# Products of the v and output projections that hand over PSUM banks run two token tiles at a time

## The chip, the cores and the metric

The kernel runs on one core of one Trainium2 chip. The metric is the device time of one execution in microseconds (us). Inside a core, TensorE (PE) multiplies matrices into PSUM banks, VectorE (DVE), ScalarE (ACT) and GpSimd (POOL) work on tiles, and SyncE (SP) issues most of the DMAs. Each engine takes its instructions in one fixed order and stops at the first one whose inputs or buffers are not ready.

## The reference

One layer of a decoder over 1024 tokens of width 2048: a projection into head groups, sparse attention (group A), mLSTM (group B), the projection of both groups' outputs, and a normalisation. The two parts that the change touches are the columns `v_m` of the first projection and the product with `w_out`:

```python
proj = x @ w_in[l]
(q_a, c_kv, z_a, q_i, k_i, w_i, q_m, k_m, v_m,
 i_m, f_m, o_m, z_m) = jnp.split(proj, offs, axis=-1)
...
h_m = mlstm_chunkwise(q_m.reshape(B, T, H_M, DK_M), k_m.reshape(B, T, H_M, DK_M),
                      v_m.reshape(B, T, H_M, DV_M), i_m + b_igate[l], f_m + b_fgate[l])
...
y = jnp.concatenate([y_a, y_m], axis=-1) @ w_out[l]
x = layer_norm(ALPHA * x + y, ln_g[l], ln_b[l])
```

## The kernel before

Every float32 factor is split into a high part (`wh`, `xh`; a cast to fp32r on ScalarE) and a low part (`wl`, `xl`; a subtraction on VectorE), and three matmuls (high x high, low x high, high x low) stand for one product of 128 x 128 by 128 x 512.

**v.** `Values` computes the 1024 x 1024 block v = x times 2048 rows of weights. `run(False)` takes the first half of the 2048 rows and `run(True)` the second, each as a scheme with seven products instead of eight for 2 x 2 blocks of 512: `b11`, `b21`, `t1`, `t2`, `b22`, `t3`, `t4`, in that order. The factor is a block of weights or a sum of blocks: `t` is a buffer of four weight tiles to which a block is added on VectorE (L847) before `t2` and again before `t4`. Each product is 4 weight tiles (k) x 4 tiles of 128 tokens (t) x 3 matmuls = 48 matmuls at L861, into four PSUM banks, one per token tile. The banks are `pj` (for b11, t2, t3, t4), `pb` (b21) and `pc` (t1, b22); pb and pc are taken from the same four banks. After a product, `add` empties its banks into `v`, by ScalarE copies in the first pass where the block is new and by VectorE additions (L889) otherwise. So t1 can begin only when the additions of pb are done, and t4 when those of t3's pj are.

`product` has two orders. With `by_tile` it asks for all four weights and then runs tile after tile; without, it runs weight after weight, and for each weight all four tiles. b11 and t4 run by tile.

There are four buffers each for `wh` and `wl` (`WB`), and six for `wraw`, the weights as loaded (`WR`).

Beside this VectorE has a search for the attention's threshold and the mask built from it: an equality test `eq` (L653), a scan (L656) and three more passes (L659, L662, L666) for each block of 128 queries, whose length grows from 384 to 1024.

**Output projection.** `Product` does the same with `w_out` and the rows of y: three units of seven products (`unit_0`, `unit_1`, `unit_2`) at L1489, banks `lps`, `pb` and `pc`, additions into `z` at L1521 and L1523, ScalarE copies and scalings at L1525 and L1527. The y factors (`ya11`, `ys1`, `ys2` and others) are also split, by L108 on ScalarE and L109 on VectorE. Here b21 and t4 run by tile.

What each engine does first is settled by a scheduler that goes over the whole program with priorities (`urgent`, `out_prio`) and an estimate of each instruction's time, and writes out one order for each engine. A change of the order in which a product asks for its matmuls therefore moves instructions on the other engines too.

Of the kernel before, what the change touches and what calls it, by code (L numbers as in the profile page):

```python
# [102 lines left out]
def kernel(ctx, tc, a, out):  # L103
# [90 lines left out]
    def bank(name, shape=(P, 512)):  # L194
        return ss.tile(list(shape), F32, name=name, tag="b")
# [45 lines left out]
    for k in range(4):  # L241
        r, ws, xs = {}, [], []
# [154 lines left out]
    w, low = {}, {}  # L397
# [49 lines left out]
    with tc.high_priority(offset=I_PRIO), tc.issue_after(marks[n + 42].ins):  # L447
        for h in range(2):
            ps = bank("knt")
# [20 lines left out]
    with tc.high_priority(offset=I_PRIO), tc.issue_after(marks[n + 46].ins):  # L470
        for j in range(2):
            cn = s4("cn")
            for h in range(2):
                ps = bank("cnt")
# [6 lines left out]
        for h in range(2):  # L481
            ps = bank("gnt")
# [211 lines left out]
    class Unit:  # L694
# [53 lines left out]
        def product(self, ps, wname, xname, start):  # L748
            wh, wl = self.weights(wname)
            fh, fl = self.X[xname]  # L750
            for k in range(4):
                for n, (w, x) in enumerate(((wh, fh), (wh, fl), (wl, fh))):
                    last_mm[0] = pe.matmul(ps, w[:, k], x[:, k], start=start and k == 0 and n == 0,  # L753
                                           stop=k == 3 and n == 2, skip_group_check=True)
                if k % 2:
                    marks.append(last_mm[0])
# [57 lines left out]
    class Values:  # L814
# [11 lines left out]
        def run(self, second, X):  # L826
            k0 = 8 * second
            t_sum = x_tile("t", dt=F32)
            with urgent():
                for k in range(4):  # L830
                    self.load(t_sum[:, k], k0 + k, 1, (k0 + k, 0))

            def raw(k, n, more=None):
                return self.load(wp.tile([P, 512], F32, name="wraw", tag="wraw", bufs=WR), k, n, more)

            def weights(name, k):
                with urgent():
                    if name in ("b11", "b21"):
                        src = raw(k0 + 4 * (name == "b21") + k, 0)
                    elif name == "b22":  # L840
                        src = raw(k0 + 4 + k, 1)
                    elif name == "t3":
                        src = raw(k0 + 4 + k, 1, (k0 + k, 1))
                    else:
                        src = t_sum[:, k]
                        if name != "t1":
                            vec.tensor_tensor(src, src, raw(k0 + 4 + k, int(name == "t2")), op=OP.add)  # L847
                    wh = wp.tile([P, 512], F32R, name="wh", tag="wh", bufs=WB)
                    wl = wp.tile([P, 512], F32R, name="wl", tag="wl", bufs=WB)
                    last_cast[0] = act.copy(wh, src)  # L850
                    last_low[0] = vec.tensor_tensor(wl, src, wh.bitcast(F32), op=OP.subtract)
                search_on()
                return wh, wl

            def product(ps, wname, xname, start, by_tile=False):
                fh, fl = X[xname]

                def part(t, k, w):
                    ts = slice(t * P, (t + 1) * P)
                    for n, (x, y) in enumerate(((fh, w[0]), (fl, w[0]), (fh, w[1]))):  # L860
                        last_mm[0] = pe.matmul(ps[t], x[:, k, ts], y, start=start and k == 0 and n == 0,  # L861
                                               stop=k == 3 and n == 2, skip_group_check=True)
                    if t % 2:
                        marks.append(last_mm[0])

                if by_tile:
                    ws = [weights(wname, k) for k in range(4)]
                    for t in range(4):
                        for k in range(4):
                            part(t, k, ws[k])  # L870
                else:
                    for k in range(4):
                        w = weights(wname, k)
                        for t in range(4):
                            part(t, k, w)

            def block(i, n):
                self.c[i, n] = [s4("v", (P, 2, 512)) for _ in range(2)]
                if second:
                    with urgent():  # L880
                        for v in range(2):
                            sync.dma_start(self.c[i, n][v], v_d[n, i, :, 2 * v:2 * v + 2])

            def add(i, n, ps, first=False, minus=False, last=False):
                for t in range(4):
                    dst = self.c[i, n][t // 2][:, t % 2]
                    with urgent():
                        if not first or second:
                            vec.tensor_tensor(dst, dst, ps[t], op=OP.subtract if minus else OP.add)  # L889
                        elif minus:  # L890
                            act.mul(dst, ps[t], -1.0)
                        else:
                            act.copy(dst, ps[t])
                    if last and t % 2:
                        sync.dma_start(v_d[n, i, :, t - 1:t + 1], self.c[i, n][t // 2])

            pa = [pj() for _ in range(4)]
            block(0, 0)
            product(pa, "b11", "a11", True, True)
            add(0, 0, pa, True)  # L900
            pb = [bank("pb") for _ in range(4)]
            block(1, 1)
            product(pb, "b21", "a12", True)
            add(0, 0, pb, last=True)
            pc = [bank("pc") for _ in range(4)]
            product(pc, "t1", "s1", True)
            add(1, 1, pc, True)
            block(0, 1)
            product(pa, "t2", "s2", False)
            add(0, 1, pa, True, True)  # L910
            product(pc, "b22", "s4", False)
            add(0, 1, pc, last=True)
            block(1, 0)
            product(pa, "t3", "s3", False)
            add(1, 1, pa, minus=True, last=True)
            product(pa, "t4", "a22", False, True)
            add(1, 0, pa, True, last=True)


# [344 lines left out]
    with ExitStack() as ph:  # L1264
# [14 lines left out]
        for t in range(7, -1, -1):  # L1279
            w = max((t + 1) * P, 256)  # L1280
# [5 lines left out]
        for t in range(8):  # L1286
            m = mask[t]
            w = max((t + 1) * P, 256)
# [146 lines left out]
    class Product:  # L1435
# [44 lines left out]
                    pool.dma_start(src, a["wo"][c, :, k0 + 4], accum_op=OP.add)  # L1480
            return wh, wl

        def product(self, ps, wname, xname, start, by_tile=False):
            fh, fl = Y[xname]

            def part(t, k, w):
                ts = slice(t * P, (t + 1) * P)
                for n, (x, y) in enumerate(((fh, w[0]), (fl, w[0]), (fh, w[1]))):
                    pe.matmul(ps[t], x[k][:, ts], y, start=start and k == 0 and n == 0,  # L1489
                              stop=k == 3 and n == 2, skip_group_check=True)  # L1490

            with tc.issue_after(last_logit[0].ins):
                if by_tile:
                    ws = [self.weights(wname, k) for k in range(4)]
                    for t in range(4):
                        for k in range(4):
                            part(t, k, ws[k])
                else:
                    for k in range(4):
                        w = self.weights(wname, k)  # L1500
                        for t in range(4):
                            part(t, k, w)

        def block(self, i, n):
            if self.p:
# [29 lines left out]
        def run(self, then, following=None):  # L1535
            pa = [lps() for _ in range(4)]
            self.block(0, 0)
            self.product(pa, "b11", "a11", True)
            self.add(0, 0, pa, True, True)
            then("a11")  # L1540
            pb = [bank("pb") for _ in range(4)]
            self.product(pb, "b21", "a12", True, True)
            self.add(0, 0, pb, last=True)
            then("a12")
            self.block(1, 1)
            pc = [bank("pc") for _ in range(4)]
            self.product(pc, "t1", "s1", True)
            self.add(1, 1, pc, True)
            then("s1")
            self.block(0, 1)  # L1550
            self.product(pa, "t2", "s2", False)
            self.add(0, 1, pa, True)
            then("s2")
            self.product(pc, "b22", "s4", False)
            self.add(0, 1, pc, last=True)
            then("s4")
            nxt = following and Product(*following)
            self.block(1, 0)
            self.product(pa, "t3", "s3", False)
            self.add(1, 1, pa, last=True)  # L1560
            then("s3")
            self.product(pa, "t4", "a22", False, True)
            self.add(1, 0, pa, True, True, last=True)
            then("a22")
            return nxt
# [47 lines left out]
    for t in range(8):  # L1613
# [5 lines left out]
        for n in range(2):  # L1619
            ps = bank("zps") if t % 2 else lps()  # L1620
# [59 lines left out]
```

## Time and profile before

| | |
|---|---|
| median of 3 runs | 1834.79 us (1834.2 to 1838.15) |
| the profiled execution | 1842.1 us |
| its span (first to last instruction) | 1840.3 us |
| granted TensorE clock, mean | 0.99 |

The span is the time between the first and the last instruction of the profiled execution; 1.8 us of its time lie outside. Times in the rows further down count from the span's start. "Idle before" is the time that an engine did nothing ahead of an instruction, and behind the arrow stands what ended it.

### The profile page before, as it was taken

To read this page: it belongs to the slowest core of one execution; us is meant where nothing else is said; L and a number is where in the kernel's file an instruction comes from. 1 tells how busy PE (TensorE), PEld (TensorE's weight loads), DVE (VectorE), ACT (ScalarE), POOL (GpSimd) and SP (SyncE) were. 2 spreads that over 40 slices of the span, in tenths; PEclk is the share of its full clock that TensorE was granted. 3 is DMA by queue.
4 is the path that set the end of the run, shared out by engine and by line. 5 is a ranking of instruction groups with operands and counts; after the bars stand their busy time and mean duration, and the time that the engine had idled before them with its cause. 6 is when DMAs were issued, how large, how long until landed. Compare 5 with 4: busy or idle time off the path is not lost. (4 is left out here: it accounts for less than half of the span.)

```text
span 1840.3 us, 25485 instructions
## 1 busy us (share of the span) xinstructions
PE 1779.2 (97%) x8613; PEld 1497.0 (81%) x8613; DVE 1400.6 (76%) x2674; ACT 942.4 (51%) x1728; POOL 263.9 (14%) x316
## 2 busy tenths in 40 slices
PE   8899999999999999999999998999899999999997
PEld 8788888887888888777888887878788987888886
DVE  8766677767887768786878786877898976676777
ACT  6343266556666657321555564565665665333410
POOL 3101110000100010000101010010445531011000
PEclk9999999999999999999999999999999999999998
DMA  9886264445475667975666656466675448874764
GB/s 327 321 294 195 86 169 116 111 122 144 132 202 152 163 169 241 306 229 159 200 179 179 204 144 179 113 196 186 215 222 141 125 107 238 264 189 121 191 183 147
DMA packets 148732, 338.82 MB, mean 184 GB/s; under 512 B 16104, under 2 KB 25576, under 8 KB 142456
## 3 DMA queue, kind: packets, MB, share of 16 engines
q1 hardware_dynamic: 121880, 280.16, 46.1%
q0 software_dynamic: 26720, 57.03, 16.4%
q8 instruction: 68, 1.11, 0.2%
q14 instruction: 64, 0.52, 0.1%
HBM read 259.40 MB, written 91.35 MB: 191 GB/s over the span
## 5 line engine op out<-in xcount | busy, mean ns | idle before, releaser
L753 PE MATMUL pj<-xh,wh 128*128 128x512 f32 x960 | 376.3, 393 | 6.3 <-DVE res L762 4.5
L753 PE MATMUL pj<-xl,wh 128*128 128x512 f32 x960 | 375.2, 391 | 0.0
L753 PE MATMUL pj<-xh,wl 128*128 128x512 f32 x960 | 371.0, 392 | 1.5 <-DVE wl L744 1.5
L743 ACT CAST wh<-wraw 128x512 fp32r<-128x512 f32 x280 | 172.3, 619 | 212.1 <-PE pj L753 95.1
L744 DVE TENSOR_TENSOR wl<-wraw,wh 128x512 fp32r<-128x512 f32 x280 | 191.8, 688 | 48.3 <-ACT wh L743 42.3
L753 PEld LDWEIGHTS pj<-xh,wh 128*128 128x128 f32 x960 | 180.6, 188 | 45.4 <-ACT wh L743 3.7
L753 PEld LDWEIGHTS pj<-xh,wl 128*128 128x128 f32 x960 | 180.4, 188 | 38.4 <-DVE wl L744 2.6
L753 PEld LDWEIGHTS pj<-xl,wh 128*128 128x128 f32 x960 | 180.5, 188 | 34.5
L722 POOL DMA_DIRECT2D wraw<-wg x80 | 68.2, 856 | 759.4 <-DMA wraw<-wg 262.1
L762 DVE TENSOR_TENSOR res<-res,pj 128x512 f32<-128x512 f32 x160 | 109.1, 682 | 54.4 <-PE pj L753 42.5
L583 DVE SCALAR_TENSOR_TENSOR sc<-r,wi,sc 128x384 f32<-128x384 f32 (+2 forms) x90 | 84.1, 947 | 31.0 <-ACT r L578 30.3
L578 ACT ACTIVATE r<-sc 128x384 f32<-128x384 f32 (+3 forms) x160 | 79.3, 524 | 51.8 <-PE sc L577 37.4
L614 ACT ACTIVATE junk<-sc,cand 128x512 bf16<-128x512 f32 (+2 forms) x93 | 86.7, 933 | 6.0 <-DVE cand L629 6.0
L108 ACT CAST wh<-wraw 128x512 fp32r<-128x512 f32 (+2 forms) x88 | 50.0, 577 | 75.8 <-PE lps L1489 20.9
L617 DVE TENSOR_SCALAR_CACHE_REDUCE junk<-sc,cand 128x384 bf16<-128x384 f32 (+2 forms) x93 | 80.0, 875 | 0.9
L1321 POOL TENSOR_TENSOR nm<-mask,tb 128x256 f32<-128x256 bf16 (+3 forms) x64 | 66.7, 1121 | 83.7 <-DVE mn L1328 70.9
L109 DVE TENSOR_TENSOR wl<-wraw,wh 128x512 fp32r<-128x512 f32 (+2 forms) x88 | 56.4, 645 | 26.2 <-ACT wh L108 17.4
L753 PE MATMUL pb<-xh,wh 128*128 128x512 f32 x160 | 63.0, 394 | 0.0
L753 PE MATMUL pb<-xh,wl 128*128 128x512 f32 x160 | 62.7, 392 | 0.2 <-DVE wl L744 0.2
L753 PE MATMUL pb<-xl,wh 128*128 128x512 f32 x160 | 62.4, 390 | 0.0
L1333 ACT ACTIVATE lg<-lg,mn 128x256 f32<-128x256 f32 (+3 forms) x64 | 50.4, 791 | 13.9 <-DVE mn L1328 13.9
L341 PE MATMUL pj<-xh,wh 128*128 128x512 f32 x128 | 51.4, 401 | 6.3 <-ACT wh L108 5.2
(561 smaller groups left out, 4483.4 us busy)
## 6 DMA issues: line engine op xcount, KB each, us to landing
wraw<-wg SPq DMA_DIRECT2D x232, 256.0 KB, 4.1
wraw<-wg POOLq DMA_DIRECT2D x80, 256.0 KB, 4.8
part_d<-res SPq DMA_DIRECT2D x20, 1024.0 KB, 4.8
res<-part_d SPq DMA_DIRECT2D x19, 1024.0 KB, 8.4
wraw<-wo SPq DMA_DIRECT2D x64, 256.0 KB, 3.6
wraw<-wv SPq DMA_DIRECT2D x48, 256.0 KB, 5.6
v_d<-v SPq DMA_DIRECT2D x16, 512.0 KB, 3.6
z<-x SPq DMA_DIRECT2D x16, 512.0 KB, 5.8
```

The source lines that it names most:

```text
L109: vec.tensor_tensor(lo, src, hi.bitcast(F32), op=OP.subtract)
L341: last_mm[0] = pe.matmul(ps[u], w[:, k], x[:, k], start=start and k == 0 and n == 0, stop=k == 3 and n == 2, skip_group_check=True)
L578: act.activation(r[:, s], ps, AF.Relu)
L583: vec.scalar_tensor_tensor(out=sc[t], in0=r, scalar=wcol, in1=sc[t], op0=OP.mult, op1=OP.add)
L614: act.activation(junk, sc[t], AF.Sign, scale=-1.0, bias=th[:, t - 2:t - 1], accum_out=cnt[:, t - 2:t - 1])
L617: vec.tensor_scalar(junk, sc[t], th[:, t - 2:t - 1], 0.0, op0=OP.is_lt, op1=OP.add, accum_out=cnt[:, t - 2:t - 1])
L722: pool.dma_start(r, a["wg"][self.g + more[1], :, k0:k0 + 4, :], accum_op=OP.add)
L743: last_cast[0] = act.copy(wh, src)
L744: last_low[0] = vec.tensor_tensor(wl, src, wh.bitcast(F32), op=OP.subtract)
L753: last_mm[0] = pe.matmul(ps, w[:, k], x[:, k], start=start and k == 0 and n == 0, stop=k == 3 and n == 2, skip_group_check=True)
L762: vec.tensor_tensor(dst, dst, ps, op=OP.subtract if minus else OP.add)
L1321: last_sum[0] = pool.tensor_tensor(nm[:, 0:ws], mask[t][:, w - ws:w], tb[:, off:off + ws], op=OP.add)
```

## The change

`by_tile` becomes `group`, the number of token tiles that run together: for each group of tiles, weight after weight, and for each weight the tiles of the group. Four is the old order without `by_tile`, one would be the old order with it. The products that take banks from another product or give them to one (b11, b21, t1, t3, t4, in both projections) get 2; t2 and b22 keep 4. A weight is loaded and split when the first group comes to it.

```diff
-            def product(ps, wname, xname, start, by_tile=False):
+            def product(ps, wname, xname, start, group=4):
...
-                if by_tile:
-                    ws = [weights(wname, k) for k in range(4)]
-                    for t in range(4):
-                        for k in range(4):
+                ws = {}
+                for t0 in range(0, 4, group):
+                    for k in range(4):
+                        if not t0:
+                            ws[k] = weights(wname, k)
+                        for t in range(t0, t0 + group):
                             part(t, k, ws[k])
-                else:
-                    for k in range(4):
-                        w = weights(wname, k)
-                        for t in range(4):
-                            part(t, k, w)
...
-            product(pa, "b11", "a11", True, True)
+            product(pa, "b11", "a11", True, 2)
...
-            product(pb, "b21", "a12", True)
+            product(pb, "b21", "a12", True, 2)
...
-            product(pc, "t1", "s1", True)
+            product(pc, "t1", "s1", True, 2)
...
-            product(pa, "t3", "s3", False)
+            product(pa, "t3", "s3", False, 2)
             add(1, 1, pa, minus=True, last=True)
-            product(pa, "t4", "a22", False, True)
+            product(pa, "t4", "a22", False, 2)
...
-            self.product(pa, "b11", "a11", True)
+            self.product(pa, "b11", "a11", True, 2)
...
-            self.product(pb, "b21", "a12", True, True)
+            self.product(pb, "b21", "a12", True, 2)
...
-            self.product(pc, "t1", "s1", True)
+            self.product(pc, "t1", "s1", True, 2)
...
-            self.product(pa, "t3", "s3", False)
+            self.product(pa, "t3", "s3", False, 2)
...
-            self.product(pa, "t4", "a22", False, True)
+            self.product(pa, "t4", "a22", False, 2)
```

The method of `Product` changes in the same way. The lines behind the first `product` move up by three (L889 becomes L886), those behind the second by six. The orders of the engines differ in the v stage and in the output projection and nowhere else; GpSimd's does not differ at all. Three places:

VectorE in the second pass of v, where b21 ends and t1 begins, before the change (`pb` are b21's banks, `wl<-t` the low parts of t1's weights, `t<-t,wraw` the sums for t2):

```order
L847 TENSOR_TENSOR t<-t,wraw 128x512
L851 TENSOR_TENSOR wl<-t,wh 128x512
L847 TENSOR_TENSOR t<-t,wraw 128x512
L851 TENSOR_TENSOR wl<-t,wh 128x512
L889 TENSOR_TENSOR v<-v,pb 128x512
L847 TENSOR_TENSOR t<-t,wraw 128x512
L889 TENSOR_TENSOR v<-v,pb 128x512 x2
L656 SCALAR_TENSOR_TENSOR pre<-one_col,eq 128x512
L889 TENSOR_TENSOR v<-v,pb 128x512
L851 TENSOR_TENSOR wl<-t,wh 128x512
```

and after it:

```order
L851 TENSOR_TENSOR wl<-t,wh 128x512
L886 TENSOR_TENSOR v<-v,pb 128x512
L847 TENSOR_TENSOR t<-t,wraw 128x512
L886 TENSOR_TENSOR v<-v,pb 128x512
L851 TENSOR_TENSOR wl<-t,wh 128x512 x2
L847 TENSOR_TENSOR t<-t,wraw 128x512
L886 TENSOR_TENSOR v<-v,pb 128x512
L847 TENSOR_TENSOR t<-t,wraw 128x512
L886 TENSOR_TENSOR v<-v,pb 128x512
L851 TENSOR_TENSOR wl<-t,wh 128x512
```

The first addition of pb now stands ahead of the first sum shown and the second between two sums; all four stand ahead of the scan.

VectorE in the same pass, where t3 ends and t4 begins, before (`pj` are the banks of t3, which t4 takes over; `wl<-t` are t4's weights):

```order
L851 TENSOR_TENSOR wl<-t,wh 128x512
L653 TENSOR_SCALAR eq<-sc_2183,thr 128x1024
L851 TENSOR_TENSOR wl<-t,wh 128x512
L656 SCALAR_TENSOR_TENSOR pre<-one_col,eq 128x1024
L889 TENSOR_TENSOR v<-v,pj 128x512 x4
L851 TENSOR_TENSOR wl<-t,wh 128x512
L659 SCALAR_TENSOR_TENSOR pre<-pre,need,eq 128x1024
L662 SCALAR_TENSOR_TENSOR pre<-sc_2183,thr,pre 128x1024
```

and after:

```order
L851 TENSOR_TENSOR wl<-t,wh 128x512
L666 TENSOR_SCALAR m<-pre 128x896
L886 TENSOR_TENSOR v<-v,pj 128x512 x2
L851 TENSOR_TENSOR wl<-t,wh 128x512
L653 TENSOR_SCALAR eq<-sc_2183,thr 128x1024
L851 TENSOR_TENSOR wl<-t,wh 128x512
L886 TENSOR_TENSOR v<-v,pj 128x512
L656 SCALAR_TENSOR_TENSOR pre<-one_col,eq 128x1024
L886 TENSOR_TENSOR v<-v,pj 128x512
L851 TENSOR_TENSOR wl<-t,wh 128x512
L659 SCALAR_TENSOR_TENSOR pre<-pre,need,eq 128x1024
L662 SCALAR_TENSOR_TENSOR pre<-sc_2183,thr,pre 128x1024
```

Two additions have moved ahead of the equality test, the third ahead of the scan, and the fourth stands behind it.

ScalarE in unit 0 of the output projection, from the last casts of y parts to the weights of t1 (`wh<-t_sum` at L108) and the first of t2 (L1427), with numbered buffers, before:

```order
L108 CAST ys2h_14747<-u_14746 128x512
L108 CAST ys4h_14762<-t_14761 128x512 x2
L108 CAST ys2h_14747<-u_14746 128x512
L108 CAST ys4h_14762<-t_14761 128x512
L108 CAST wh_14974<-t_sum_14722 128x512
L108 CAST ys2h_14747<-u_14746 128x512
L108 CAST wh_14992<-t_sum_14722 128x512
L108 CAST ys2h_14747<-u_14746 128x512
L108 CAST wh_15010<-t_sum_14723 128x512
L108 CAST ys4h_14762<-t_14761 128x512
L108 CAST wh_15028<-t_sum_14723 128x512
L1427 ACTIVATE wh_15051<-t_sum_14722 128x512
```

and after (it starts with the cast of t1's first weight; ahead of it stand one cast of ys2h and one of ys4h):

```order
L108 CAST wh_14974<-t_sum_14722 128x512
L108 CAST ys4h_14762<-t_14761 128x512
L108 CAST ys2h_14747<-u_14746 128x512
L108 CAST wh_14986<-t_sum_14722 128x512
L108 CAST ys4h_14762<-t_14761 128x512
L108 CAST ys2h_14747<-u_14746 128x512
L108 CAST wh_14998<-t_sum_14723 128x512
L108 CAST ys2h_14747<-u_14746 128x512
L108 CAST ys4h_14762<-t_14761 128x512
L108 CAST wh_15010<-t_sum_14723 128x512
L108 CAST ys3h_14777<-u_14776 128x512 x2
L1424 ACTIVATE wh_15051<-t_sum_14722 128x512
```

t1's first cast now has three casts of y parts fewer ahead of it, the second two fewer and the third one, and two ys3h casts have come ahead of t2's first weight.

## Rows read from the trace of the kernel before

**Rows 1.** The page's busy times: us, share of the span, instructions.

```profile
PE 1779.2 (97%) x8613; PEld 1497.0 (81%) x8613; DVE 1400.6 (76%) x2674; ACT 942.4 (51%) x1728; POOL 263.9 (14%) x316
```

**Rows 2.** Stretches: us, busy us of each engine, clock, DMA share, GB/s.

```profile
670.00:861.00 191.00, 182.64 (x780) 148.35 (x779) 150.13 (x264) 78.52 (x137) 17.22 (x20) 0.97 0.80 244
786.30:789.80 3.50, 3.16 (x8) 2.52 (x9) 3.50 (x6) 0.00 (x0) 0.00 (x0) 0.51 0.87 268
834.00:841.00 7.00, 5.75 (x14) 4.58 (x15) 6.67 (x9) 0.00 (x0) 0.00 (x0) 0.51 0.95 289
```

**Rows 3.** Matmuls of line L861: idle time before them, then who waited for them.

```profile
  DVE v L889: 7.2, 5
...
  ACT wh L850: 5.0, 6
...
  ACT wh L850: 51.5, 20
```

**Rows 4.** Timeline of TensorE, second v pass: start, us, work [idle before <-releaser].

```profile
759.72 0.39 PE L861 MATMUL pj<-wh,xl 128*128 128x512 f32 x1
759.95 0.39 PE L861 MATMUL pj<-wl,xh 128*128 128x512 f32 x1
761.23 0.50 PE L861 MATMUL pj<-wh,xh 128*128 128x512 f32 x1 [0.90 <-ACT wh L850]
...
781.25 0.50 PE L861 MATMUL pb<-wh,xh 128*128 128x512 f32 x1 [0.67 <-ACT wh L850]
...
786.64 0.77 PE L861 MATMUL pc<-wh,xh 128*128 128x512 f32 x1 [2.33 <-DVE v L889]
787.20 0.63 PE L861 MATMUL pc<-wh,xl 128*128 128x512 f32 x1
787.63 0.63 PE L861 MATMUL pc<-wl,xh 128*128 128x512 f32 x1
...
835.25 0.77 PE L861 MATMUL pj<-wh,xh 128*128 128x512 f32 x1 [3.37 <-DVE v L889]
```

**Rows 5.** Timeline of VectorE, second v pass, the same columns.

```profile
784.60 0.69 DVE L847 TENSOR_TENSOR t<-t,wraw 128x512 f32<-128x512 f32 x1 [0.71 <-DMA wraw<-wv]
...
785.81 0.68 DVE L889 TENSOR_TENSOR v<-v,pb 128x512 f32<-128x512 f32 x1
...
787.01 1.28 DVE L889 TENSOR_TENSOR v<-v,pb 128x512 f32<-128x512 f32 x2
...
796.35 0.69 DVE L851 TENSOR_TENSOR wl<-t,wh 128x512 fp32r<-128x512 f32 x1 [1.38 <-ACT wh L850]
...
819.18 0.69 DVE L847 TENSOR_TENSOR t<-t,wraw 128x512 f32<-128x512 f32 x1 [2.80 <-DMA wraw<-wv]
...
820.39 2.02 DVE L656 TENSOR_TENSOR_SCAN pre<-one_col,eq 128x896 f32<-128x896 f32 x1
...
823.51 0.69 DVE L851 TENSOR_TENSOR wl<-wraw,wh 128x512 fp32r<-128x512 f32 x1
...
832.24 2.28 DVE L656 TENSOR_TENSOR_SCAN pre<-one_col,eq 128x1024 f32<-128x1024 f32 x1
834.44 2.45 DVE L889 TENSOR_TENSOR v<-v,pj 128x512 f32<-128x512 f32 x4
```

**Rows 6.** Timeline of TensorE in the output projection, units 0, 0 and 1.

```profile
1530.76 0.50 PE L1489 MATMUL pc<-wh,ys1h 128*128 128x512 f32 x1 [1.93 <-ACT wh L108]
...
1573.29 0.50 PE L1489 MATMUL lps<-wl,ys3h 128*128 128x512 f32 x1 [0.69 <-DVE wl L109]
...
1653.33 0.47 PE L1489 MATMUL lps<-wh,ya22h 128*128 128x512 f32 x1 [0.78 <-DVE z L1521]
```

**Rows 7.** Timeline of ScalarE around t1 and t2 of the output projection's unit 0.

```profile
1529.57 0.62 ACT L108 CAST ys4h<-t 128x512 fp32r<-128x512 f32 x1 [1.04 <-DMA t<-y_form_d0s]
1530.09 0.61 ACT L108 CAST wh<-t_sum 128x512 fp32r<-128x512 f32 x1
...
1538.99 0.62 ACT L108 CAST ys3h<-u 128x512 fp32r<-128x512 f32 x1 [1.20 <-DMA u<-y_form_d0s]
```

More of the change, by code (lines that the diff above doesn't have):

```diff
@@ L1481, in weights, with product @@
             return wh, wl
-        def product(self, ps, wname, xname, start, by_tile=False):
+        def product(self, ps, wname, xname, start, group=4):
             fh, fl = Y[xname]
@@ L1492, in product @@
             with tc.issue_after(last_logit[0].ins):
[L1493 to L1496, printed above, removed]
-                            part(t, k, ws[k])
[L1498 to L1502, printed above, removed]
+                ws = {}
+                for t0 in range(0, 4, group):
+                    for k in range(4):
+                        if not t0:
+                            ws[k] = self.weights(wname, k)
+                        for t in range(t0, t0 + group):
+                            part(t, k, ws[k])
         def block(self, i, n):
```

## The prediction

> **What bounds the kernel now.** I read the busy times first. TensorE is busy 1779.2 of 1840.3 us [rows 1], so time can only go where TensorE waits or runs at its lower clock. Next the stretches: between 670 and 861 us, where v is projected, the granted clock averages 0.97, and it is 0.51 in two short stretches, 786.3 to 789.8 and 834 to 841 us [rows 2], the lower level of 1.2 GHz. Then the waits of the v matmuls' line: 7.2 us in five waits end with the VectorE addition that reads a bank out (v L889), 5.0 us with ScalarE's cast of a weight [rows 3]. Last the timeline, to place them. At full clock matmuls start 0.23 us apart (759.72, 759.95 [rows 4]), so a product of 48 takes 11.0 us; at the lower clock it is 0.43 us (787.20, 787.63). A matmul lasts 0.39 us but the next starts after 0.23, so a wait costs 0.16 us more than its printed idle time; I add that below.
>
> The two large waits are in the second pass: t1 starts 2.33 us late at 786.64, t4 3.37 us late at 835.25 [rows 4], and each time the clock falls behind the wait. Both wait for additions that VectorE has in its queue behind other work. For t1, a sum t += wraw that waited 0.71 us for its load comes first, and the first pb addition runs only at 785.81 [rows 5]. For t4 it is the 2.28 us scan at 832.24; the four pj additions start at 834.44 [rows 5].
>
> **The change, part by part.** No matmul, cast, split, sum, addition or load is added or taken away; the same instructions come in another order. With group 2 tiles 0 and 1 are complete about halfway through a product, 24 matmuls or 5.5 us before its end, and tiles 2 and 3 of the next product are first wanted 5.5 us after its start. In return all four weights are wanted in the first half.
>
> First pass. The five L889 waits less 2.33 and 3.37 leave 1.5 us in three [rows 3, 4]. The new VectorE order puts those additions at the places they had, so I take only 0.2 us of it (0 to 1.5).
>
> The Trainium skill ("Perfetto Trace Analysis", section Matmuls) says that independent groups should rotate through different PSUM banks, so that reading one out overlaps the matmuls of the next. By that rule alone every hand-over wait would go, and the sum below would be about 1.3 us larger. The trace differs: the banks alternated before as well, and what was late was the addition's place in VectorE's queue [rows 5].
>
> Second pass, b11: 0.90 us before 761.23 ends with the cast of wh [rows 4]. That cast now comes first on ScalarE, but the copies that empty banks 2 and 3 of the last product come behind casts, and I work out a wait of about 1.25 us there from that queue's steps of 0.52 us (1529.57 to 1530.09 [rows 7]): -0.2 (-1.3 to +1.1).
>
> b21: the last weight ended a wait of 0.67 us at 781.25 [rows 4]. Its load is now issued next to that of the weight before it, ahead of a large load of res: 0.67 + 0.16, +0.8.
>
> t1: in the new VectorE order the addition of pb bank 0 stands ahead of the first sum, and that of bank 1 between the first sum and the next. The wait goes, 2.33 + 0.16 = 2.5, and with it the lower clock: seven matmuls at 0.43 instead of 0.23 us, 1.4. Together +3.9. The lo-split of t1's last weight now follows two more sums; counting VectorE's pieces from the first sum at 0.6 us each and waiting for each sum's load as before, I put its end at 788.1 us against a demand at 787.6: -0.5.
>
> t3: here group 2 costs something. The lo-split of its third weight started at 823.51 and ended at 824.2, behind a sum that waited 2.80 us for its load and a 2.02 us scan [rows 5]. t3 began at 835.25 - 3.37 - 11.0 = 820.9. In the new order that split is wanted 15 matmuls in, at +3.4, so 824.3: no wait if TensorE were not ahead. But TensorE comes here ahead by 0.8 + 3.9 - 0.5 - 0.2 + 0.2, some 4.2 to 4.6 us. How far VectorE moves up decides. It has 1.38 us of idle time at 796.35 to give back [rows 5], and the splits that stood behind b21's late weight start some 1.5 us sooner: about 3 us, and the loads it triggers move with it. Wait: 4.5 - 3.0 = 1.5 us, so -1.5. Bounds: 0, and -4.5 if the chain of sums and loads does not move at all; a wait that long would bring the lower clock again, for -2.8 more by what it cost behind the 3.37 us.
>
> t4: additions of pj banks 0 and 1 now stand ahead of the 128x1024 equality test and the scan, that of bank 2 between them, that of bank 3 behind the scan; banks 2 and 3 are wanted only 5.5 us into t4. The wait goes, 3.37 + 0.16 = 3.5, and 14 matmuls [rows 2] at 0.43 instead of 0.23 us, 2.8: +6.3 (3.5 if the clock falls anyway).
>
> v stage: 0.2 - 0.2 + 0.8 + 3.9 - 0.5 - 1.5 + 6.3 = 9.0 us. What follows (the next units' products at L753) keeps its order on every engine, and TensorE bounds it, so I let the lead stand.
>
> Output projection. Unit 0's t1 waited 1.93 us for a cast [rows 6] that stood on ScalarE behind casts of ys2 and ys4 that wait for loads [rows 7]. In the new order the casts of wh stand among them earlier, and 2.1 us go. But t2's first cast now stands behind two ys3h casts, the first of which waited for a load until 1538.99 [rows 7]: about 1.2 us come back. Then t3 waits at 1573.29 for the lo-split of its last weight [rows 6], which follows sums that wait for loads; this does not move, only two fewer matmuls are left after it, 0.45 us. So unit 0 gives 0.5, whatever t1 gains. Unit 1's t4 waited 0.78 us for an addition [rows 6]; with two banks free early I take 0.5. Unit 2: nothing. Together +1.0 (-2 to +3).
>
> Sum: 10.0 us. The profiled execution took 1842.1 us, 1.8 more than its span, and would become 1832.1. It is 7.3 above the median 1834.8 of the runs shown; I take the same saving there: **1824.8 us**.
>
> **The rivals.**
>
> A. VectorE and its loads hold the second pass, and t3 gives the lead back. For it: splits of t3 came with little to spare and behind waits of 1.38 and 2.80 us [rows 5]. Against it: part of that idle time is a wait for ScalarE's cast, which follows TensorE. It gives 10.0 - 3.0 - 2.8 = 4.2: 1830.6.
>
> B. Slower: there are four buffers each for wh and wl. In group 4 the first weight's pair is free after 12 of 48 matmuls, which leaves 36 x 0.23 = 8.2 us for the next product's cast and split; in group 2 it is free after about 27, which leaves 4.8. ScalarE's casts already wait for TensorE's release, 51.5 us in 20 waits [rows 3]. Cast and split take 0.62 + 0.69 us; if VectorE or ScalarE then has more than 3.5 us of other work ahead (scans of 2.28 do that together with additions), TensorE waits. Fifteen products go from 4 to 2. From 0.7 us each this decides; at 1 us it gives 1834.8 - 10 + 15 = 1840. Against it: products that ran one tile at a time kept their buffers still longer, and only one of them, b11, shows a wait of this kind.
>
> C. No change: the v stage's lead is lost where later stages wait for loads, not for TensorE. Against it: 97% busy [rows 1]. Of 10.0 some 2 would be left: 1833.
>
> D. The waits go but the low-clock stretches stay: 10.0 - 4.2 = 5.8, 1829. For it: nothing but that the clock also falls elsewhere in this trace; against it, both stretches begin at a long wait [rows 2, 4]. The Trainium skill ("TensorE: Matmul & The Clock Gate", section Loop structure matters more than you think) says that dense matmuls stay warm and long waits between them make the clock fall; by that the clock comes back with the waits, and these rows agree.
>
> **How the numbers follow.** Forecast 0.50, A 0.24, B 0.10, C 0.10, D 0.06. About 0.2% (3.7 us) is what a measurement can tell from no change here. Faster: forecast, D and most of A, 0.76. Same: C and the rest of A, 0.14. Slower: 0.10. Lower end: no t3 and t1 waits (+2.0) and the output projection at its bound (+2): 1820.5. Upper end: A with the output projection at its lower bound, 10.0 - 5.8 - 3.0 = 1.2: 1833. B lies outside.
>
> **What would show it.** Right: no wait over 0.7 us at the starts of t1 and t4 in the second pass, clock 1.0 there, the pj additions of t3 in two groups around the scan, and a wait of 1 to 2 us inside t3 for wl. The v stage ends about 9 us earlier against its start, the output projection is about 1 us shorter. Wrong: a clock of 0.5 inside t3 (A), waits for wh at the starts of many products (B), or a lead that the trace shows at 861 us but not at 1480 us (C).

## The result, and the profile after

The changed kernel takes 1828.79 us (median of 7 runs, 1825.02 to 1831.09) against 1838.15 us of the kernel before in the same comparison (1834.03 to 1841.0): the ratio is 0.9948, 95% interval 0.9933 to 0.9963, a gain of 9.4 us. A second comparison on another occasion gave 0.9952 (0.9939 to 0.9966), 9.6 us. The forecast was a gain of 10.0 and, from the median of 1834.79 that was known then, a time of 1824.8 us; the measured time is 4.0 us longer, and 3.4 of these are the kernel before, which came out at 1838.15 here.

Where it came from is read in the same views as before. The stretches of the changed kernel (columns as in [rows 2]; the v stage now ends ten microseconds earlier, so the windows move with it; the third is in the output projection):

```profile
670.00:851.00 181.00, 176.97 (x776) 144.77 (x775) 149.34 (x262) 78.16 (x134) 16.60 (x20) 1.00 0.83 256
826.00:833.00 7.00, 7.00 (x33) 5.79 (x32) 7.00 (x10) 1.25 (x2) 0.19 (x1) 1.00 0.94 219
1529.00:1533.00 4.00, 4.00 (x12) 3.19 (x11) 3.21 (x7) 4.00 (x9) 0.00 (x0) 0.58 0.27 104
```

The v stage runs at the full clock now (it was 0.97), and so do the 7 us around the start of t4 in the second pass (0.51 before). A stretch of lower clock has appeared in the output projection, where there was none. Then the waits of the v matmuls' line, which answer to [rows 3]:

```profile
  ACT v L890: 5.9, 5
  DVE wl L851: 1.4, 2
  DVE v L886: 1.1, 2
...
  ACT wh L850: 1.0, 2
```

This view adds the idle time ahead of a weight load to that of the matmul behind it, so its sums are above what TensorE lost: of the 7.2 us in five [rows 3], the matmuls' own waits are 6.8 in four (0.66, 0.42, 2.33 and 3.37), and of the 5.9 us now, 2.4 in two. The additions (now L886) cost the matmuls 1.1 us in two waits, both in the first pass. What ends most of the idle time now is ScalarE's copy out of a bank (v L890). TensorE's timeline shows where (against [rows 4] and [rows 6]):

```profile
759.99 0.50 PE L861 MATMUL pj<-wh,xh 128*128 128x512 f32 x1 [0.69 <-ACT v L890]
...
762.95 0.49 PE L861 MATMUL pj<-wh,xh 128*128 128x512 f32 x1 [1.75 <-ACT v L890]
...
783.69 0.39 PE L861 MATMUL pb<-wl,xh 128*128 128x512 f32 x1
783.91 0.39 PE L861 MATMUL pc<-wh,xh 128*128 128x512 f32 x1
...
816.55 0.39 PE L861 MATMUL pj<-wh,xh 128*128 128x512 f32 x1
...
820.62 0.50 PE L861 MATMUL pj<-wl,xh 128*128 128x512 f32 x1 [0.50 <-DVE wl L851]
...
828.00 0.39 PE L861 MATMUL pj<-wl,xh 128*128 128x512 f32 x1
828.23 0.39 PE L861 MATMUL pj<-wh,xh 128*128 128x512 f32 x1
...
1528.42 0.50 PE L1486 MATMUL lps<-wh,ys2h 128*128 128x512 f32 x1 [1.82 <-ACT wh L1424]
```

t1 begins at 783.91, t3 at 816.55 and t4, 48 matmuls later, at 828.23; t1 and t4 start 0.23 us behind the matmul before them, with no wait at all. b11 of the second pass waits twice, 0.69 and 1.75 us, for copies. t3 waits 0.50 us inside for a low part. In unit 0 of the output projection it is now t2 that waits, 1.82 us. VectorE's timeline (against [rows 5]):

```profile
780.72 0.69 DVE L886 TENSOR_TENSOR v<-v,pb 128x512 f32<-128x512 f32 x1
781.32 0.69 DVE L847 TENSOR_TENSOR t<-t,wraw 128x512 f32<-128x512 f32 x1
781.92 0.68 DVE L886 TENSOR_TENSOR v<-v,pb 128x512 f32<-128x512 f32 x1
...
815.54 0.69 DVE L847 TENSOR_TENSOR t<-t,wraw 128x512 f32<-128x512 f32 x1 [4.21 <-DMA wraw<-wv]
...
826.73 1.28 DVE L886 TENSOR_TENSOR v<-v,pj 128x512 f32<-128x512 f32 x2
...
829.80 0.68 DVE L886 TENSOR_TENSOR v<-v,pj 128x512 f32<-128x512 f32 x1
830.39 2.29 DVE L656 TENSOR_TENSOR_SCAN pre<-one_col,eq 128x1024 f32<-128x1024 f32 x1
```

The first pb addition runs at 780.72, ahead of the first sum and three microseconds ahead of the start of t1. Two pj additions run at 826.73, while t3 is still computing its other two banks; the third stands ahead of the 2.29 us scan. The sum that t3 depends on came at 815.54 instead of 819.18; the stage itself began 0.7 us earlier in this trace, so it moved up 2.9 us against the stage's start. ScalarE in unit 0 (against [rows 7]):

```profile
1526.10 0.62 ACT L108 CAST ys3h<-u 128x512 fp32r<-128x512 f32 x1 [6.36 <-DMA u<-y_form_d0s]
1527.22 0.62 ACT L108 CAST ys3h<-u 128x512 fp32r<-128x512 f32 x1 [0.50 <-DMA u<-y_form_d0s]
1527.74 0.62 ACT L1424 ACTIVATE wh<-t_sum 128x512 fp32r<-128x512 f32 x1
```

t2's first cast (L1424) stands behind two ys3h casts, of which the first waited 6.36 us for its load.

Lengths of the stages come from the first and last starts that the view of a line gives. For v's matmuls these are 676.5 and 848.7 us before:

```profile
L861 PE MATMUL pj<-wh,xh x128: 389/389/767, 676.5 to 848.3; 128*128 128x512 f32 x128
...
L861 PE MATMUL pj<-wl,xh x128: 388/389/632, 677.4 to 848.7; 128*128 128x512 f32 x128
```

and 675.8 and 838.9 after:

```profile
L861 PE MATMUL pj<-wh,xh x128: 388/389/500, 675.8 to 838.4; 128*128 128x512 f32 x128
...
L861 PE MATMUL pj<-wl,xh x128: 388/389/500, 676.7 to 838.9; 128*128 128x512 f32 x128
```

In the two profiled executions: v stage 172.2 us before and 163.1 after; from there to the first matmul of the output projection 646.2 and 642.7; from there to the end of the span 345.4 and 345.4; before the v stage 676.5 and 675.8. The spans differ by 13.3 us, more than the medians. The middle stretch has the same order of instructions in every kernel of this study, and it lasted between 640.1 and 646.2 us in them; so its 3.5 us are scatter. Between these two traces the v stage is what the change moved; the output projection came out equal.

### The profile page after: what moved, and what is told of

It reads as the page before. It is cut to its first block, busy times and chain, and to the rows that moved or that the text cites. A ratio compares the mean times of both kernels' runs of the same rounds, so it can differ in the third digit from the quotient of the medians.

```text
span 1827.0 us, 25483 instructions
## 1 busy us (share of the span) xinstructions
PE 1774.0 (97%) x8613; PEld 1493.9 (82%) x8613; DVE 1400.2 (77%) x2674; ACT 943.5 (52%) x1728; POOL 263.5 (14%) x316
## 5 line engine op out<-in xcount | busy, mean ns | idle before, releaser
L743 ACT CAST wh<-wraw 128x512 fp32r<-128x512 f32 x280 | 172.2, 619 | 207.8 <-PE pj L753 92.3
L108 ACT CAST wh<-wraw 128x512 fp32r<-128x512 f32 (+2 forms) x88 | 50.2, 575 | 80.3 <-PE lps L1486 22.6
```

## The experiments

Every kernel ran five rounds beside the kernel before on the same chip. A ratio below one is faster than the kernel before.

**The v projection alone.** The output projection gets its old groups back (`b11` 4, `b21` 1, `t1` 4, `t3` 4, `t4` 1):

```diff
-            self.product(pa, "b11", "a11", True, 2)
+            self.product(pa, "b11", "a11", True)
...
-            self.product(pa, "t4", "a22", False, 2)
+            self.product(pa, "t4", "a22", False, 1)
```

> Groups of two in the v projection alone; the output projection keeps its old order. Theory (the gain is the two waits of the second v pass and the lower clock behind them): about 9 us below the kernel before, TensorE loses some 5 us between the starts of the v matmuls and their end instead of 14, and the output projection shows the old wait of 1.9 us at unit 0's t1. Rival (the output projection brings a good part): only 4 to 6 us below.

Ratio 0.9966 (0.9954 to 0.9978), 6.5 us by the medians. The v stage lasted 164.1 us, as short as in the changed kernel, and unit 0's t1 waits 1.89 us again. So the larger part is v's, but 6.5 lies nearer to the rival's number than to 9. Why is seen in the next run.

**The output projection alone.** The other half, with v's old groups (`b11` 1, `b21` 4, `t1` 4, `t3` 4, `t4` 1):

> Groups of two in the output projection alone. Theory: about 1 us below the kernel before, since the wait of 1.9 us at unit 0's t1 comes back as one of 1.8 us at t2 with a stretch of lower clock behind it; the v stage shows 2.33 and 3.37 us as before. Rival (the output projection brings a good part): 4 us below or more.

Ratio 0.9990 (0.9976 to 1.0005), 1.4 us by the medians: in size what the theory said, and too small to tell from nothing. t2 waits 1.28 us, without the stretch of lower clock that the theory had. This run also shows v's old order once more: its waits were 2.01 us at t1, without a stretch of lower clock behind it, and 2.86 us at t4, and the stage lasted 169.4 us, not 172.2. The same order thus costs 3 us less or more from one execution to the next, and the trace that the forecast was made on was a long one. A v gain of 9.1 us between two traces and of 6 to 7 us between medians fit together. TensorE at t1 and t4 in this run:

```profile
785.35 0.47 PE L861 MATMUL pc<-wh,xh 128*128 128x512 f32 x1 [2.01 <-DVE v L886]
...
832.00 0.52 PE L861 MATMUL pj<-wh,xh 128*128 128x512 f32 x1 [2.86 <-DVE v L886]
```

The traces of all runs with the same order say the same. v's old order lasted 172.2 and 169.4 us, the new one 163.1 to 164.3 in five traces, about 7.1 less on average. The output projection lasted 345.4 to 350.4 us in the five traces with its old order and 344.8 to 347.6 in the five with the new one, 1.9 less on average, against a scatter of 5 within one order.

**Only t3 in twos.** In v `t3` has 2, all else is as before:

```diff
-            product(pa, "t3", "s3", False)
+            product(pa, "t3", "s3", False, 2)
```

> Only t3 of the v projection runs in groups of two (t4 stays one tile at a time, all else as before). Theory (the product that hands its banks over decides, since two of its banks are free half a product earlier): t4's wait of 3.37 us and its stretch of lower clock are gone, t1's 2.33 us and its stretch stay; about 6 us below the kernel before. Rival (both products need the new order): t4 still waits 2 us or more, gain under 3 us.

Ratio 0.9974 (0.9960 to 0.9987), 4.3 us. Waits of TensorE in the v stage (engine, line, waited for, us in total, times, longest):

```profile
PE pc L861 <- DVE v L886: 3.6, 2, 2.3
...
PE pj L861 <- DVE v L886: 0.4, 1, 0.4
```

The waits for pj are down to 0.4 us: t4 starts without one although it runs one tile at a time. t1's wait (pc, longest 2.3) and a low clock behind it are still there. VectorE's timeline where t3 ends:

```profile
831.77 1.28 DVE L886 TENSOR_TENSOR v<-v,pj 128x512 f32<-128x512 f32 x2
...
833.57 0.75 DVE L653 TENSOR_SCALAR eq<-sc,thr 128x1024 bf16<-128x1024 f32 x1
...
834.83 0.69 DVE L886 TENSOR_TENSOR v<-v,pj 128x512 f32<-128x512 f32 x1
835.43 2.29 DVE L656 TENSOR_TENSOR_SCAN pre<-one_col,eq 128x1024 f32<-128x1024 f32 x1
```

Two additions run ahead of the equality test and the third ahead of the scan. These three are all that stands elsewhere in VectorE's order, by the two traces; ScalarE's and GpSimd's orders are the same as before. So the product that hands its banks over decides, as the theory had it, and by the medians this one argument is worth most of the v gain (4.3 of 6.5 us). The rival falls.

**Only b21 and t1 in twos.**

```diff
-            product(pb, "b21", "a12", True)
+            product(pb, "b21", "a12", True, 2)
...
-            product(pc, "t1", "s1", True)
+            product(pc, "t1", "s1", True, 2)
```

> Only b21 and t1 of the v projection run in groups of two. Theory: t1's wait of 2.33 us and its low clock are gone and so is the wait inside b21, 4.7 us up to there; t4 still waits, since its additions stand behind the scan as before. If VectorE's work moves up with TensorE, 4 to 5 us below the kernel before. Rival (VectorE's chain is pinned by its own work and loads): t4's wait grows from 3.4 to 5 us or more and only 1 to 3 us are left.

Ratio 1.0006 (0.9992 to 1.0020): nothing. TensorE's timeline at t1 and t4:

```profile
786.37 0.47 PE L861 MATMUL pc<-wh,xh 128*128 128x512 f32 x1 [1.44 <-DVE v L886]
...
834.17 0.76 PE L861 MATMUL pj<-wh,xh 128*128 128x512 f32 x1 [4.02 <-DVE v L886]
```

and VectorE's ahead of t4:

```profile
831.15 2.30 DVE L656 TENSOR_TENSOR_SCAN pre<-one_col,eq 128x1024 f32<-128x1024 f32 x1
833.35 2.47 DVE L886 TENSOR_TENSOR v<-v,pj 128x512 f32<-128x512 f32 x4
```

t1's wait shrinks to 1.44 us (its additions have moved, but here two sums still stand ahead of the first), and t4's grows from 3.37 to 4.02, with the lower clock behind it. The theory's 4.7 us up to t1 were never won: b11, whose order is the old one here, waited 2.03 us instead of 0.90 in this trace. Against the stage's start t1 began 0.5 us later than before; with no lower clock behind t1, t3 then began 0.9 us earlier. The scan started only 0.3 us earlier against the stage's start, and t4's longer wait took back two thirds of the 0.9. In direction this is the rival of the expectation (its 5 us were not reached), and rival A of the prediction in small: what stands behind the scan sets the start of t4, and time won ahead of it is waited away there. How a full lead of 4 us at this place would have fared was not measured.

**The scan behind the additions, no twos.** All groups as in the kernel before; the search's steps get an order edge behind the last addition (`last_add` is set by `add`):

```diff
-            with tc.issue_after(last_cast[0].ins), tc.issue_after(last_low[0].ins):
-                next(steps, None)
+            with tc.issue_after(last_cast[0].ins), tc.issue_after((last_add[0] or last_low[0]).ins):
+                with tc.issue_after(last_low[0].ins):
+                    next(steps, None)
```

> The kernel before with no group of two anywhere; only the steps of the search are put behind the additions of the product before them on VectorE, so that t4's additions precede the 128x1024 equality test and scan. Theory of place (what counts is that the additions come ahead of the scan): t4's wait falls from 3.4 us to about 1 us and its low clock goes, 4 us below the kernel before. Rival (the banks must be free half a product earlier): t4 still waits 2 us or more, and the gain is under 2 us.

Ratio 0.9968 (0.9956 to 0.9981), 4.8 us. VectorE where t3 ends:

```profile
828.88 2.48 DVE L887 TENSOR_TENSOR v<-v,pj 128x512 f32<-128x512 f32 x4
831.27 0.62 DVE L666 TENSOR_SCALAR m<-pre 128x896 bf16<-128x896 f32 x1
831.81 0.75 DVE L653 TENSOR_SCALAR eq<-sc,thr 128x1024 bf16<-128x1024 f32 x1
```

and TensorE's waits in the v stage:

```profile
PE pj L862 <- DVE v L887: 2.7, 1, 2.7
PE pc L862 <- DVE v L887: 1.9, 2, 1.0
```

All four additions run ahead of the equality test (831.81) and the scan, and t4 of the second pass has no wait worth a row; the 2.7 us for pj belong to t4 of the first pass, where two counting passes of the search (L605, 1.14 and 1.28 us) stand in the way: they ran ahead of b22's additions before, and the new edges put them between those and t3's. The clock fell there. Even so the stage lasted 164.5 us, against 164.1 with twos in v. The edges moved more than the scan (t1's wait also fell, to 1.0 us), but t4's wait has gone with no group of two at all. With the run of t3 alone this shows the cause of that wait: the place of the additions in VectorE's queue. Running two tiles at a time is one way to get them there.

**ys3 and ya22 of unit 0 behind t2's casts**, in the changed kernel (`last_neg` is the last cast of `split_minus`):

```diff
-    for name in ("s1", "s2", "s4", "s3", "a22"):
+    for name in ("s1", "s2", "s4"):
         next_form(0)(name)
-    unit_1 = unit_0.run(lambda name: None, (0, 1))
+    def rest(name):
+        if name == "s2":
+            with tc.issue_after(last_neg[0].ins):
+                next_form(0)("s3")
+                next_form(0)("a22")
+
+    unit_1 = unit_0.run(rest, (0, 1))
```

> The changed kernel, with the splits of ys3 and ya22 in unit 0 put behind t2's four casts on ScalarE. Theory (the wait of 1.8 us at t2 and the low clock behind it come from two ys3h casts that stand ahead of t2's first cast): both go, about 3 us below the changed kernel, so 12 us below the kernel before. Rival (VectorE's chain pins t3 of unit 0): t3's wait of 0.6 us grows to 3 us or more and the time stays within 1 us of the changed kernel.

Ratio 0.9963 (0.9949 to 0.9978), not below the changed kernel, whose ratios are 0.9948 and 0.9952 in the two comparisons that have it. t2's wait is gone, but t4 now waits, by TensorE's timeline

```profile
1561.20 0.77 PE L1488 MATMUL lps<-wh,ya22h 128*128 128x512 f32 x1 [3.59 <-ACT wh L108]
```

and ScalarE's shows why:

```profile
1556.52 0.62 ACT L108 CAST ys1h<-u 128x512 fp32r<-128x512 f32 x1 [8.36 <-DMA u<-y_d]
1558.51 0.62 ACT L108 CAST ys1h<-u 128x512 fp32r<-128x512 f32 x1 [1.37 <-DMA u<-y_d]
1559.04 1.13 ACT L108 CAST wh<-t_sum 128x512 fp32r<-128x512 f32 x2
```

The clock fell at this wait. t4's first cast (wh<-t_sum at 1559.04) stands behind two ys1h casts of the next unit, of which one waited 8.36 us for its load. It is the same pattern one place on. The time is the rival's, the mechanism is not: neither sums nor low parts held t3, but ScalarE's queue held t4.

**b11 and t4 of v one tile at a time again**, in the changed kernel:

```diff
-            product(pa, "b11", "a11", True, 2)
+            product(pa, "b11", "a11", True, 1)
...
-            product(pa, "t4", "a22", False, 2)
+            product(pa, "t4", "a22", False, 1)
```

> The changed kernel, with b11 and t4 of the v projection one tile at a time again (b21, t1, t3 stay in twos). Theory (the second pass's b11 lost 1.7 us because in twos it wants banks 2 and 3 while their copies wait on ScalarE behind casts): the waits of 0.7 and 1.75 us at its start become one of 0.9 to 2, some 1 us below the changed kernel, and t4's hand-over stays without a wait, since t3 alone decides it. Rival (t4 in twos is needed): t4 waits over 1 us again and the time is above the changed kernel's.

Ratio 0.9966 (0.9951 to 0.9982). t4's hand-over has no wait, so twos are not needed there. But b11's start did not get better: it waited 4.00 us in the profiled execution, with a stretch of lower clock at its end, while ScalarE's queue stood behind a cast of x that had waited 2.09 us for its load.

**These two edits together.**

> Both edits together: b11 and t4 of v one tile at a time, ys3 and ya22 behind t2's casts in unit 0. If the theories of the two hold: 13 us below the kernel before, 4 us below the changed kernel.

Ratio 0.9953 (0.9936 to 0.9969), 6.8 us: no better than the changed kernel, as the two runs before it let expect.

The last four ran in one comparison. **The changed kernel once more:**

> The changed kernel once more, beside the three that follow: 9 us below the kernel before (ratio 0.995).

Ratio 0.9952 (0.9939 to 0.9966), 1830.68 us.

**b11's later casts behind the copies** (second pass; `last_copy` is set by `add`):

```diff
-                    last_cast[0] = act.copy(wh, src)
+                    if name == "b11" and second and k:
+                        with tc.issue_after(last_copy[0].ins):
+                            last_cast[0] = act.copy(wh, src)
+                    else:
+                        last_cast[0] = act.copy(wh, src)
```

> The changed kernel, with the casts of b11's second to fourth weight in the second v pass put behind the four copies that empty t4's banks on ScalarE. Theory (the 1.75 us at 762.95 is the copy of bank 2 standing behind two casts): that wait goes to 0.5 us or less, the v stage loses some 2 us less, 1.5 to 2 us below the changed kernel. Rival (VectorE's low parts and the chain behind them set b11's pace): the wait moves into b11's matmuls that use wl and less than 0.5 us is gained.

Ratio 0.9954 (0.9939 to 0.9969), 1830.66 us: no change. TensorE at b11's start:

```profile
762.88 0.50 PE L865 MATMUL pj<-wh,xh 128*128 128x512 f32 x1 [1.77 <-ACT v L894]
...
764.80 0.58 PE L865 MATMUL pj<-wh,xh 128*128 128x512 f32 x1 [0.70 <-ACT v L894]
...
766.28 1.22 PE L865 MATMUL pj<-wl,xh 128*128 128x512 f32 x2 [0.47 <-DVE wl L855]
```

The wait for bank 2's copy, 1.75 us in the changed kernel, is down to 0.70, as the theory had it. But the one ahead of b11's first matmul has grown from 0.69 to 1.77, a low part costs 0.47, and the clock was 0.51 from 765.0 to 768.5; the v stage lasted 166.4 us in this trace. Ahead of the copies stands a cast of x that waits for its load: 3.49 us in the changed kernel's first trace, 2.09 in the run with b11 one tile at a time, 2.08 here. Against the stage's start it began 1.4 us later here than in the changed kernel's first trace. So ScalarE's whole queue comes late here. That those loads are the cause was not tried.

**ys3, ya22 and the next unit's ys1 behind the weight casts** (the edit of the run that moved ys3, and):

```diff
-    unit_1.run(next_form(1))
+    t4_cast = last_split[0]
+
+    def form_1(name):
+        with tc.issue_after(t4_cast.ins):
+            next_form(1)(name)
+
+    unit_1.run(form_1)
```

> The changed kernel, with the splits of ys3 and ya22 behind t2's casts and those of unit 1's ys1 behind t4's casts of unit 0. Theory (weight casts stand behind casts of y parts that wait for loads, at t2 first and at t4 once t2 is cured): no wait over 0.7 us at either place, no low clock between 1480 and 1600 us, the output projection loses some 4 us less than in the run that moved ys3 and ya22 alone, 3 to 4 us below the changed kernel. Rival (loads bound unit 0): the wait appears at the next product that needs a load, unit 1's t1 or b11, and the time stays within 1 us of the changed kernel.

Ratio 0.9937 (0.9922 to 0.9953), 1827.22 us, 3.5 us below the changed kernel in the same comparison. The stretch with unit 0 and the start of unit 1, in one window:

```profile
1480.00:1600.00 120.00, 120.00 (x592) 101.48 (x591) 80.06 (x145) 55.36 (x105) 16.64 (x19) 1.00 0.71 215
```

TensorE is busy for all of the 120 us and its clock is 1.00. From the first output matmul to the end of the span it took 340.1 us, against 346.0 in the changed kernel beside it. The two intervals overlap, but the traces agree: the output projection lasted 340.1 us in both traces with this edit and at least 344.8 in every trace without any edit of these casts. The theory holds: casts of weights stood behind casts that wait for loads, first at t2, then at t4.

**Both edits together.**

> The edits of the two runs before it together. If both theories hold, 5 us below the changed kernel, 14 to 15 below the kernel before.

Ratio 0.9935 (0.9922 to 0.9947), 1827.47 us: the same as with the late y parts alone. b11's wait for bank 2 is again 0.70 us, and here it is the only one:

```profile
762.30 0.50 PE L867 MATMUL pj<-wh,xh 128*128 128x512 f32 x1 [0.70 <-ACT v L896]
```

The run before it had two, of 0.80 and 1.73 us. But b21 then waits 0.80 us for a cast and t1 1.09 us for an addition, and the v stage lasts 164.1 us against 164.3: what was won at b11 is waited away at the next two products. These two runs are the fastest kernels of the study.

## Why the prediction was right, step by step

**What bounds the kernel, and which waits.** Right. The two waits of the second pass and the clock behind them went, in the way that was read from the order: additions in pairs, ahead of the sums and of the scan. For t4 the runs with t3 alone and without twos confirm the reason, the place in VectorE's queue; for t1 it rests on the traces alone. That the banks alternated before is wrong for these two hand-overs: t1 took the four banks that b21 had just filled, and t4 those of t3, so there was no other bank to go on with. Groups of two let two of the four be emptied while the other two are in use.

**The terms of the v stage.** Between the two traces the sum is 9.1 us where 9.0 were forecast, but the terms are not those. By the starts of the products, against the stage's start:

- First pass: 0.3 us won, 0.2 forecast. The waits of 0.67 us at t1 and 0.42 at t4 stayed. Of the 1.5 us that the prediction saw there, 1.1 are the matmuls' own.
- b11 was mis-sized: 0.2 us lost were forecast, with 1.3 as the worst case; 1.06 us became 0.85 + 1.9 by starts, 1.7 lost.
- b21's late weight: right, 0.8.
- t1: wait and lower clock gone, 4.1 us won where 3.9 were forecast, and t1's last low part caused no wait (0.5 had been taken off).
- t3 lost 0.8 us where 1.5 were forecast. Its rule was right: VectorE moved up 2.9 us (3.0 forecast). But TensorE arrived only 3.6 us early instead of 4.5, because b11 had lost more, so there was less lead to wait away. The wait of 1 to 2 us that was named as a sign did not come; it was 0.50.
- t4: wait and lower clock gone, 6.3 us, as forecast.

b11 came out 1.5 us worse than forecast, and what was better at t1 (0.7 us, with its last low part) and t3 (0.7) made up for it. Part of that follows from b11's loss, since a TensorE that comes later waits less for VectorE; that the whole came out so close is luck.

**That the terms add.** This step was weaker than the sum looks. By the medians b21 and t1 alone gain nothing, t3 alone 4.3 us, and both with the rest 6.5. That is no clean test of t1's 3.9 us, since with b21 and t1 alone most of t1's wait stayed. But it shows, as does the last run, that an earlier term can be taken back by a later wait. The prediction used this for t3 (how far VectorE moves up) but not in the way it listed the other terms side by side.

**The output projection.** 1.0 us was forecast; 1.4 us between medians when changed alone, with an interval that holds zero, and none between the two traces (345.4 and 345.4). The path was as told, t1's wait gone and t2's come instead, but that was 1.8 us, not 1.2, in this trace, and with a stretch of lower clock, which the forecast did not have (1.20 to 1.57 us without one in four other traces). Waits in units 1 and 2 went altogether (0.78 and 0.53 us before) and made up for it.

**The saving on the median.** The forecast took the saving of one trace as that of the median. The old v stage lasted 172.2 us in that trace and 169.4 in the other that has it, so a part of the 9.0 was the chance of that execution; that the whole still came out at 9.4 to 9.6 is partly luck. v alone gave 6.5 by the medians and the output projection alone 1.4; the averages over traces, 7.1 and 1.9, come to 9.0. So v gave some 2 us less than forecast and the output projection perhaps 1 us more. The range's lower end is mis-added as well: its own terms give 1820.8, not 1820.5.

**The rivals.** A is real as a mechanism (only b21 and t1 in twos) but not here, since t3 moves the additions. B did not occur: in the same view, idle time that ended with a cast of one of v's weights fell from 5.0 us [rows 3] to 1.0. C: the lead was not lost in the middle. D: the clock came back with the waits, 1.00 over the whole v stage.

## What to carry to other kernels

When an engine waits for a bank to be emptied, look at what stands ahead of the emptying instruction in its queue before making it faster: two tiles at a time, or an order edge that puts the search behind it, gave the same v stage. Look at the last wait of a chain first: t3 alone gave 4.3 us, b21 and t1 alone nothing, and in two traces time won early was waited away at a later product. And an engine that casts both weights and data from loads, in one queue, should have the weights ahead: the wait of 1.8 us came back as one of 3.6 at the next such place until both were moved, and only then were 3.5 us won by the medians.

## What the runs showed of the hardware

Whether the clock falls at a wait is not settled by the wait's length between 1.7 and 2.5 us. In the v stage and the output projection it fell at 1.82 us at unit 0's t2 in the changed kernel (matmuls 0.43 us apart from 1529.7 on), at 2.27 us at t1 with t3 alone in twos, and at 2.33 us in [rows 4]. It did not fall at 1.75 us at b11 in the changed kernel, nor at another wait of 1.82 us, at unit 0's t1 with b21 and t1 alone in twos (granted clock 1.00 from 1525 to 1535), nor at 2.01 us at t1 with the output projection alone changed, nor at 2.41 us at unit 0's t1 with t3 alone in twos. All six waits of 2.7 us and more there, over all runs, had a stretch at 1.2 GHz that began during the wait or right behind it. A price for the clock's fall thus belongs in a sum as a chance, not as a sure term, when the wait is about 2 us.
